# Gates kept in DRAM, high weight parts first, three weight buffers, two sums in the convolution and a new order of products in a hybrid decoder step

## The chip, the cores and the metric

The kernel runs on one core of one Trainium2 chip. The metric is the device time of one execution in microseconds (us). Five engines matter: PE (TensorE: matmuls, transposes), DVE (VectorE), ACT (ScalarE: activations, copies), POOL (GpSimd: elementwise work) and SP (SyncE: it issues nearly all DMAs, in one queue). Each runs its own instructions in order, and they wait for each other on semaphores.

## What is computed

One step of a decoder layer on 520 tokens (512 of a prompt, 8 samples), 1024 features. Three mixers run side by side on the columns of one projection, and each has a gate:

```python
h = rms_norm(x, g_mix)
proj = jnp.einsum('ntd,de->nte', h, w_in)
u_a, z_b, u_c, gate_in = ...                       # 1024, 1024, 512, 3072 columns
c_a, new_conv_a = causal_dwconv(u_a, conv_a, w_conv_a, b_conv_a)          # width 4
y_a, new_h = rg_lru(c_a, h_a, ...)                                         # A: gated recurrence
glu_b = z_b[..., :W_B] * jax.nn.sigmoid(z_b[..., W_B:])
c_b, new_conv_b = causal_dwconv(glu_b, conv_b, w_dw_b, b_dw_b)             # B: width 31
y_b = jax.nn.silu(layer_norm(c_b, ln_g_b, ln_b_b))
y_c, ... = s5_ssm(u_c, s_re, s_im, ...)                                    # C: diagonal SSM, then GLU
```

Each y is projected to 1024 features (w_pa, w_pb, w_pc), multiplied by sigmoid(gate_in + b_gate) of its branch, and the three are added. Then come w_out, the residual, RMSNorm, a SwiGLU FFN of width 2816 with its residual, and a last RMSNorm.

## The kernel before

**Layout and products.** Features lie on the 128 partitions, the 520 tokens on the free axis, as two halves of 260 columns. Both operands of a large product are split exactly into a high and a low part in float32r, and three products are added: high weight by high input, high weight by low input, low weight by high input. `prod` (L232) goes over the k tiles of 128 rows; for each it calls `prod1` (L240), which issues the three products for two halves: 6 matmuls per k, 48 for 8 k tiles, 24 for 4 (L244). One such group makes one tile of 128 output columns in a PSUM tile of the pool mm, which has three.

**Weights.** `wcol` loads two column tiles with one DMA on SP's queue (`wload`, L209, 1 MB, two buffers wraw). `wsplit` makes whi on ACT (L216) and wlo on DVE or, for the keys in ON_POOL, on POOL (L217). There are two whi and two wlo buffers, so a tile can be split only when the product two before is done.

**Steps.** The order of TensorE's work is written by hand in the string ORDER (L43); each word calls a function of the table `step`. DVE, ACT, POOL and SP are ordered by a scheduler, by priorities. The words:
- b0.*, b1.*: first products of branch B and its GLU, which fill the convolution's inputs `gext`. bs: states of the samples. bc.t: the convolution of tile t (`b_conv`, called by `b_low` with the lowest priority).
- cp, cq, cr, cd, cm, ci, co: the S5 recurrence in four groups ct. cr transposes coefficients (L841), cd and cm make and shift the products inside a chunk (L876), ci enters the chunk inputs (L887) and starts the recurrence on DVE, co makes outputs (L951). gelu and glu end branch C; ct transposes C (L720), s0 the samples' states.
- a, ac, ag, ar: inputs, convolution, gates and recurrence of branch A; asp splits its outputs ya (`split`, L247 on ACT, L248 on DVE or POOL) for pa.
- gc.c, ga.c, gb.c: the 24 gate tiles (`gate`); sigmoid into a tile of four, kept in SBUF. pc.c, pa.c, pb.c: the projections (`proj`), which multiply with the gate (in place) and add to the merged sum (L1245, L1247). lnp, ln1, ln2, ln3: the layer norm of branch B.

**The convolution.** For each of four tiles `b_conv` multiplies the samples' windows (L1172), lets ACT make tap 0 into `acc`, and then runs 30 instructions on DVE (L1176), each `acc = window * weight + acc`. Tile t's sum lies in the input of the tile before it, so the order of the tiles is fixed, and the first tap waits for the mark that ci.3 sets (`b_after[0] = marks[3]`).

Of the kernel before, what the change touches and what calls it, by code (L numbers as in the profile page):

```python
# [1566 lines left out]
```

## Time and profile before

| what | value |
|---|---|
| time, median of 3 runs | 943.68 us (942.58 to 943.85) |
| span of the profiled execution | 940.4 us |
| PE busy | 864.3 us (92%), 7329 matmuls |
| DVE busy | 609.5 us (65%), 942 instructions |
| ACT busy | 347.6 us (37%) |
| POOL busy | 289.5 us (31%) |
| DMA | 87.99 MB, mean 94 GB/s |
| chain that ended last | PE 61%, DVE 12% of the span |

The span runs from the first to the last instruction of the profiled execution; the run's time holds a little more. Matmuls are pipelined, so their busy time overlaps and is no measure of pace; the pace is read from start to start, or from a long unbroken piece of the chain. A wait is the idle time of an engine before an instruction, put down to what released it. Instructions of a timeline row ("x5") follow each other without a gap.

### The profile page before, as it was taken

The numbers are of one execution on the slowest core, as the hardware profiler recorded it, in microseconds if no ns is written. First come the engines' busy times: TensorE is split into PE (matmuls) and PEld (weight loads), VectorE is DVE, ScalarE is ACT, GpSimd is POOL, SyncE is SP. The second block draws the span as 40 slices with busy tenths as digits, with TensorE's granted clock in tenths as the row PEclk, the third lists the DMA queues.
The fourth block names the chain that finished last, engine by engine and source line by source line (L and its number), as shares of the span: only waits on it lengthen the run. The fifth ranks groups of instructions, "written<-read, shape, count | busy, mean of one in ns | idle before, by whom it ended". The sixth has DMA issues, their size and how long they took to land.

```text
span 940.4 us, 17346 instructions
## 1 busy us (share of the span) xinstructions
PE 864.3 (92%) x7329; PEld 853.8 (91%) x7329; DVE 609.5 (65%) x942; ACT 347.6 (37%) x516; POOL 289.5 (31%) x363
## 2 busy tenths in 40 slices
PE   6888767957798799999999999999999999999997
PEld 5887767957798699999999999999999999999997
DVE  7899695889999999993546454444442244444453
ACT  6522234627484623223634342333321222223331
POOL 6569994648674441242121210000000000000021
PEclk9998998979799899999999999999999999999999
DMA  6814212130202032222226223333123432321232
GB/s 195 262 57 136 68 51 64 45 114 1 68 24 90 24 133 91 90 91 90 75 72 232 95 85 101 121 100 99 41 84 90 145 98 91 112 91 43 84 99 91
DMA packets 97756, 87.99 MB, mean 94 GB/s; under 512 B 7923, under 2 KB 95207, under 8 KB 97151
## 3 DMA queue, kind: packets, MB, share of 16 engines
q1 hardware_dynamic: 97343, 86.28, 28.3%
q8 instruction: 57, 0.93, 0.4%
q0 software_dynamic: 320, 0.57, 0.2%
q14 instruction: 20, 0.16, 0.1%
q10 hardware_dynamic: 16, 0.03, 0.0%
HBM read 81.23 MB, written 6.19 MB: 93 GB/s over the span
## 4 chain that ended last, share of the span: by engine, by line
PE 61%; DVE 12%; issue 1%; ACT 1%; DVEq 0%
PE mm L244 57%; DVE q L1176 4%; PE mm L1516 3%; DVE t L1176 2%; DVE h L248 1%; DVE wlo L217 1%; DVE q L1109 1%; ACT t L135 0%; DVE tx L1040 0%; DVE t L574 0%; DVE q L1110 0%; DVE q L1245 0%; PE ms L1356 0%; DVE t L1098 0%; PE mm L1187 0%
## 5 line engine op out<-in xcount | busy, mean ns | idle before, releaser
L244 PE MATMUL mm<-q,whi 128*128 128x260 f32 x3296 | 534.3, 284 | 1.6 <-ACT whi L216 1.6
L244 PEld LDWEIGHTS mm<-q,whi 128*128 128x128 f32 x3296 | 454.8, 190 | 2.0 <-ACT whi L216 1.8
L244 PE MATMUL mm<-q,wlo 128*128 128x260 f32 x1648 | 333.1, 283 | 10.1 <-DVE wlo L217 7.1
L216 ACT ACTIVATE whi<-wraw 128x1024 fp32r<-128x1024 f32 (+3 forms) x146 | 139.5, 956 | 433.1 <-PE mm L244 367.9
L244 PEld LDWEIGHTS mm<-q,wlo 128*128 128x128 f32 x1648 | 255.8, 190 | 12.0 <-DVE wlo L217 8.4
L217 DVE TENSOR_TENSOR wlo<-wraw,whi 128x1024 fp32r<-128x1024 f32 (+3 forms) x113 | 127.3, 1127 | 49.4 <-ACT whi L216 49.1
L244 PE MATMUL mm<-h,whi 128*128 128x260 f32 x800 | 130.9, 286 | 2.6 <-DVE h L248 2.5
L1388 POOL TENSOR_TENSOR t<-t,t 128x260 f32<-128x260 f32 (+1 forms) x9 | 8.8, 976 | 369.3 <-ACT t L1386 369.3
L244 PEld LDWEIGHTS mm<-h,whi 128*128 128x128 f32 x800 | 111.5, 191 | 3.1 <-DVE h L248 2.7
L217 POOL TENSOR_TENSOR wlo<-wraw,whi 128x1024 fp32r<-128x1024 f32 (+1 forms) x33 | 71.7, 2173 | 129.5 <-ACT whi L216 114.0
L244 PE MATMUL mm<-h,wlo 128*128 128x260 f32 x400 | 82.0, 287 | 6.3 <-DVE wlo L217 6.0
L244 PEld LDWEIGHTS mm<-h,wlo 128*128 128x128 f32 x400 | 62.7, 192 | 6.9 <-DVE wlo L217 6.4
L1176 DVE SCALAR_TENSOR_TENSOR q<-q,vec 128x512 f32<-128x512 f32 x60 | 59.1, 985 | 1.2
L1467 DVE TENSOR_TENSOR t<-mm,t 128x520 f32<-128x520 f32 x22 | 15.4, 699 | 67.4 <-PE mm L244 58.3
L1457 DVE TENSOR_TENSOR t<-mm,t 128x520 f32<-128x520 f32 x22 | 15.4, 700 | 63.4 <-PE mm L244 63.4
L129 ACT ACT_TABLE_LOAD x23 | 29.5, 1283 | 1.1 <-PEq L1555 0.7
L1176 DVE SCALAR_TENSOR_TENSOR t<-q,vec,t 128x512 f32<-128x512 f32 x30 | 28.4, 945 | 0.4
L1482 DVE TENSOR_TENSOR q<-mm,q 128x520 f32<-128x520 f32 x12 | 8.4, 698 | 27.9 <-PE mm L244 27.9
L1307 POOL TENSOR_TENSOR t<-t,t 128x520 f32<-128x520 f32 x7 | 12.4, 1770 | 41.7 <-ACT t L1306 41.7
L1176 DVE SCALAR_TENSOR_TENSOR q<-q,vec,q 128x512 f32<-128x512 f32 x30 | 24.3, 810 | 0.8
L1245 DVE TENSOR_TENSOR q<-mm,q 128x520 f32<-128x520 f32 x24 | 16.6, 690 | 12.1 <-PE mm L244 12.1
L135 ACT ACTIVATE t<-t,zero_t 128x520 f32<-128x520 f32 x30 | 21.2, 719 | 0.0
(422 smaller groups left out, 1001.8 us busy)
## 6 DMA issues: line engine op xcount, KB each, us to landing
wraw<-w_ffn_in SPq DMA_DIRECT2D x22, 1024.0 KB
wraw<-w_in SPq DMA_DIRECT2D x21, 1024.0 KB
wraw<-w_ffn_out SPq DMA_DIRECT2D x16, 384.0 KB
wraw<-w_ffn_out SPq DMA_DIRECT2D x16, 320.0 KB
wraw<-w_pa SPq DMA_DIRECT2D x4, 1024.0 KB
wraw<-w_out SPq DMA_DIRECT2D x4, 1024.0 KB
xT_d<-q SPq DMA_DIRECT2D x2, 1040.0 KB
q<-xT_d SPq DMA_DIRECT2D x2, 1040.0 KB
```

The costliest lines, as they stand in the source:

```text
L129: last_tab[0] = after(S.preload_act_table_set(SETS[func]), last_tab[0])
L135: last_tab[0] = after(S.activation(out, x, func, **kw), last_tab[0])
L216: S.activation(hi, raw, AF.Copy)
L217: e.tensor_tensor(lo, raw, hi.bitcast(F32), op=ALU.subtract)
L244: T.matmul(ps[:, h, 0:HN], w, x[:, h * HN:(h + 1) * HN], start=first and i == 0, stop=last and i == 2)
L248: e.tensor_tensor(lo, src, hi.bitcast(F32), op=ALU.subtract)
L1176: ins = V.scalar_tensor_tensor(pv(acc), win(k), wdw(k, t), pv(acc), op0=ALU.mult, op1=ALU.add)
L1245: V.tensor_tensor(hv(g), ev(ps), hv(g), op=ALU.mult)
L1307: G.tensor_tensor(ssum, ssum, sq, op=ALU.add)
L1457: V.tensor_tensor(hv(sl), ev(ps), hv(R2), op=ALU.mult)
L1467: V.tensor_tensor(hv(up), ev(ps), hv(R2), op=ALU.mult)
L1516: T.matmul(ps[:, 0, 0:HN], w[:, k, :], x[:, h * HN:(h + 1) * HN], start=j == 0 and k == 0 and i == 0, stop=j == 1 and k == hk - 1 and i == 2)
```

## The change

- `gate` writes its sigmoid into a tile of its own and stores it to a DRAM tensor `g_d`; `proj` loads gate tiles back, up to three ahead, and multiplies there. The merged sums get own tiles (`mg`). That makes 24 stores and 24 loads of 128x520 float32 on SP's queue. The pool of large tiles goes from 11 to 10.
- `prod` issues all products with whi first (high and low input for each k), then all with wlo.
- whi and wlo get three buffers each.
- `b_conv` keeps two sums, `acc` for even and `odd` for odd taps. ACT starts both (taps 0 and 1), DVE runs 29 taps and one add. The sums lie in spare tiles. The mark of ci.3 is no longer waited for (AFTER3 is False).
- ORDER is new: bs comes later, b1.* earlier; gc.0 to ga.5 and gb.0 to gb.5 come earlier, between the steps of S5 and ahead of pa; pb comes last without gates between.
- Code for a convolution on TensorE (CONV_PE, b_shift) is added, but CONV_PE is empty, so none of it is issued.

```diff
 ORDER = """
-bs b0.0 cp.0 as b0.1 ct s0 cp.1 ap b1.0 cr.0 b0.2 b1.1 cd.0 cq.1 ci.0 cr.1 b0.3 b1.3 cm.0 cq.0 ci.1 a.0 a.1 a.2
-ac.0 cd.1 cp.2 co.0 cq.2 ac.1 cm.1 a.3 cr.2 ag.0 co.1 cd.2 ag.1 ac.2 ar.0 b1.2 ci.2 a.4 a.5 ac.3 cm.2 cp.3 gc.0
-gc.1 cr.3 co.2 cd.3 ag.2 cq.3 cm.3 ci.3 ag.3 bc.0 ac.4 ar.1 gc.2 gc.3 ac.5 a.6 co.3 ag.4 ag.5 bc.1 ar.2 a.7 bc.2
-gc.4 bc.3 gelu gc.5 ac.6 gc.6 ag.6 glu.0 glu.1 gc.7 ac.7 glu.2 glu.3 ga.0 ag.7 ar.3 asp pc.0 ga.1 pc.1 pc.2 pc.3
-pc.4 pc.5 ga.2 ga.3 ga.4 pc.6 pc.7 ga.5 gb.0 lnp pa.0 pa.1 gb.1 pa.2 pa.3 pa.4 ga.6 pa.5 ga.7 pa.6 ln1 gb.2 gb.3
-ln2 pa.7 ln3 gb.4 gb.5 pb.0 pb.1 gb.6 gb.7 pb.2 pb.3 pb.4 pb.5 pb.6 pb.7
+b0.0 cp.0 as b0.1 ct ap s0 bs cp.1 b1.0 b1.1 cr.0 b0.2 cq.1 b0.3 ci.0 cr.1 gc.0 gc.1 cq.0 b1.2 cd.0 b1.3 cm.0 a.0 ci.1
+a.2 ac.0 a.1 cd.1 a.3 a.4 ac.1 gc.2 co.0 cp.2 gc.3 cm.1 cr.2 ag.0 cq.2 co.1 cd.2 ag.1 ac.2 ci.2 a.5 cp.3 ac.3 gc.4
+gc.5 cm.2 cr.3 co.2 cd.3 ag.2 ar.0 gc.6 gc.7 cq.3 ci.3 cm.3 ga.0 ga.1 ag.3 ga.6 ga.7 a.6 a.7 bc.0 ac.4 ac.5 ar.1 ga.2
+ga.3 ag.4 ag.5 bc.1 ar.2 bc.2 ga.4 ga.5 co.3 gb.4 ac.6 gb.5 gelu ag.6 glu.0 glu.1 ac.7 glu.2 glu.3 gb.0 gb.1 ag.7 pc.0
+pc.1 ar.3 pc.2 bc.3 pc.3 asp pc.4 pc.5 gb.2 pc.6 pc.7 gb.3 lnp pa.0 pa.1 pa.2 pa.3 ln1 gb.6 gb.7 ln2 pa.4 pa.5 pa.6
+ln3 pa.7 pb.0 pb.1 pb.2 pb.3 pb.4 pb.5 pb.6 pb.7
 """
...
-        hi, lo = dst or (wp.tile([P, nk, P], F32R, tag="whi", name=nm("whi")),
-                         wp.tile([P, nk, P], F32R, tag="wlo", name=nm("wlo")))
+        hi, lo = dst or (wp.tile([P, nk, P], F32R, tag="whi", name=nm("whi"), bufs=3),
+                         wp.tile([P, nk, P], F32R, tag="wlo", name=nm("wlo"), bufs=3))
...
-        n = len(xk)
-        for k, (xh, xl) in enumerate(xk):
-            prod1(ps, hi[:, k, :], lo[:, k, :], xh, xl, first and k == 0, last and k == n - 1)
...
+        mms = [(hi[:, k, :], x) for k, xx in enumerate(xk) for x in xx]
+        mms += [(lo[:, k, :], xx[0]) for k, xx in enumerate(xk)]
+        n = len(mms)
+        for i, (w_, x) in enumerate(mms):
             for h in range(2):
-                T.matmul(ps[:, h, 0:HN], w, x[:, h * HN:(h + 1) * HN], start=first and i == 0, stop=last and i == 2)
+                T.matmul(ps[:, h, 0:HN], w_, x[:, h * HN:(h + 1) * HN], start=first and i == 0, stop=last and i == n - 1)
...
-        S.activation(pv(acc), win(0), AF.Identity, bias=wdw(31, t), scale=wdw(0, t))
-        for k in range(1, 31):
-            ins = V.scalar_tensor_tensor(pv(acc), win(k), wdw(k, t), pv(acc), op0=ALU.mult, op1=ALU.add)
...
+            odd = tt()
+            S.activation(pv(acc), win(0), AF.Identity, bias=wdw(31, t), scale=wdw(0, t))
+            S.activation(pv(odd), win(1), AF.Copy, scale=wdw(1, t))
+            for k in range(2, 31):
+                x = pv((acc, odd)[k % 2])
+                ins = V.scalar_tensor_tensor(x, win(k), wdw(k, t), x, op0=ALU.mult, op1=ALU.add)
+                if k == 2 and t in b_after:
+                    after(ins, b_after[t])
+            ins = V.tensor_tensor(pv(acc), pv(acc), pv(odd), op=ALU.add)
...
-        tact(hv(gt[br, c // 4][:, c % 4, :]), ev(ps), AF.Sigmoid, bias=vb("b_gate", 8 * br + c))
-
-    mx = []
+        g = tt()
+        tact(hv(g), ev(ps), AF.Sigmoid, bias=vb("b_gate", 8 * br + c))
+        Y.dma_start(g_d[br, c], g)
+
+    mx, mg = [], {}
+    ahead = [(br, c) for br in (2, 0, 1) for c in range(8)]
 
     def proj(br, wname, nk, xk, c):
+        while ahead and len(gt) < 3:
+            n = ahead.pop(0)
+            gt[n] = tt()
+            Y.dma_start(gt[n], g_d[n[0], n[1]])
...
-        m, g = gt[2, c // 4][:, c % 4, :], gt[br, c // 4][:, c % 4, :]
-        V.tensor_tensor(hv(g), ev(ps), hv(g), op=ALU.mult)
+        m, g = mg[c // 4][:, c % 4, :], gt.pop((br, c))
+        V.tensor_tensor(hv(m if br == 2 else g), ev(ps), hv(g), op=ALU.mult)
```

On PE before, these rows stand from cd.1 (L863) over co.0 (L951) to cm.1 (L876, transposes of t, which POOL and DVE make from cd.1's result):

```order
L863 MATMUL ms_198_1749<-h_111_1061,q_66_683 32x128 x8
L951 MATMUL mm_211_1794<-h_129_1167 32x136 x4
L951 MATMUL mm_211_1794<-h_148_1329,h_168_1505 32x136 x8
L951 MATMUL mm_211_1794<-h_129_1167 32x128 x4
L951 MATMUL mm_211_1794<-h_148_1329,h_168_1505 32x128 x8
L951 MATMUL mm_211_1794<-h_129_1167 32x128 x4
L951 MATMUL mm_211_1794<-h_148_1329,h_168_1505 32x128 x8
L951 MATMUL mm_211_1794<-h_129_1167 32x128 x4
L951 MATMUL mm_211_1794<-h_148_1329,h_168_1505 32x128 x8
L876 MATMUL ms_221_1873<-ident_80,t_199_1758 128x128 x4
```

On PE after, directly ahead of cm.1 (now L894) stands the product of gc.3; three more whole products (a.3, a.4, gc.2) and co.0 lie between it and cd.1. These are the product's last rows, from the eighth group of its high weights on:

```order
L252 MATMUL mm_242_2205<-q_22_152,whi_240_2201 128x260 x2
L252 MATMUL mm_242_2205<-q_20_150,whi_240_2201 128x260 x2
L252 MATMUL mm_242_2205<-q_22_152,whi_240_2201 128x260 x2
L252 MATMUL mm_242_2205<-q_20_150,whi_240_2201 128x260 x2
L252 MATMUL mm_242_2205<-q_22_152,whi_240_2201 128x260 x2
L252 MATMUL mm_242_2205<-q_19_149,wlo_241_2202 128x260 x8
L252 MATMUL mm_242_2205<-q_20_150,wlo_241_2202 128x260 x8
L894 MATMUL ms_244_2257<-ident_80,t_211_1930 128x128 x4
L859 MATMUL ms_246_2264<-ident_80,h_229_2169 128x128 x4
```

Four products of 48 matmuls came between cd.1 and cm.1, and within a product wlo (the last 16 matmuls) now comes after all of whi.

On DVE before, the taps begin behind the end of ci.3 (L907); t_330 is the only sum of the first tile:

```order
L907 TENSOR_TENSOR h_319_2634<-h_316_2621 128x4x128
L1176 SCALAR_TENSOR_TENSOR t_330_2687<-q_74_808,vec_147,t_330_2687 128x2x256
L217 TENSOR_TENSOR wlo_353_2895<-wraw_351_2892,whi_352_2894 128x1024
L1176 SCALAR_TENSOR_TENSOR t_330_2687<-q_74_808,vec_147,t_330_2687 128x2x256
L1042 SCALAR_TENSOR_TENSOR t_348_2883<-q_73_802,vec_147,tx_347_2879 128x2x256
L1048 SCALAR_TENSOR_TENSOR t_348_2883<-q_73_802,vec_147,tx_347_2879 128x2x4
L1176 SCALAR_TENSOR_TENSOR t_330_2687<-q_74_808,vec_147,t_330_2687 128x2x256
```

On DVE after, the same place; t_382 and t_385 are the two sums, wlo_400 the low weights of ga.2:

```order
L227 TENSOR_TENSOR wlo_377_3262<-wraw_375_3259,whi_376_3261 128x1024
L227 TENSOR_TENSOR wlo_400_3471<-wraw_398_3468,whi_399_3470 128x1024
L1202 TENSOR_TENSOR t_383_3372<-q_72_801,vec_147 128x248
L1206 TENSOR_REDUCE t_384_3374<-t_383_3372 128x8
L1061 SCALAR_TENSOR_TENSOR t_387_3414<-q_75_804,vec_147,tx_386_3410 128x2x256
L1067 SCALAR_TENSOR_TENSOR t_387_3414<-q_75_804,vec_147,tx_386_3410 128x2x4
L1236 TENSOR_SCALAR t_382_3371<-t_384_3374,vec_147 128x2x4
L1229 SCALAR_TENSOR_TENSOR t_382_3371<-q_72_801,vec_147,t_382_3371 128x2x256
L1229 SCALAR_TENSOR_TENSOR t_385_3376<-q_72_801,vec_147,t_385_3376 128x2x256
L1229 SCALAR_TENSOR_TENSOR t_382_3371<-q_72_801,vec_147,t_382_3371 128x2x256
```

The taps alternate between two tiles, and the low weights of ga.2 stand ahead of the first.

On SP before, the loads between the weights of the RG-LRU gates (w_rg) and the projections follow each other:

```order
L1066 DMA t_397_3435<-w_rg 128x2x128
L1066 DMA t_397_3435<-w_ig 128x2x128
L209 DMA wraw_406_3462<-w_glu_c 128x4x256
L209 DMA wraw_424_3601<-w_glu_c 128x4x256
L209 DMA wraw_434_3672<-w_in 128x8x256
L209 DMA wraw_454_3802<-w_pc 128x4x256
L209 DMA wraw_464_3919<-w_pc 128x4x256
```

On SP after, the same place; g_d is the DRAM tensor of the gates:

```order
L1294 DMA g_d_813<-t_406_3580 128x520
L219 DMA wraw_464_4073<-w_glu_c 128x4x256
L219 DMA wraw_479_4158<-w_glu_c 128x4x256
L1294 DMA g_d_813<-t_432_3789 128x520
L1294 DMA g_d_813<-t_436_3846 128x520
L1294 DMA g_d_813<-t_442_3956 128x520
L219 DMA wraw_488_4228<-w_in 128x8x256
L1085 DMA t_455_4045<-w_rg 128x2x128
L1085 DMA t_455_4045<-w_ig 128x2x128
L1294 DMA g_d_813<-t_450_4025 128x520
L219 DMA wraw_505_4367<-w_pc 128x4x256
```

Stores of gates came in between, up to three ahead of one weight load.

## Rows read from the trace of the kernel before

**Rows 1.** Busy time of each engine by stretch (us, with counts), clock, DMA share, GB/s.

```profile
0.00:70.00 70.00, 56.31 (x413) 52.77 (x414) 57.89 (x245) 31.68 (x73) 43.08 (x95) 0.98 0.55 173
70.00:146.97 76.97, 54.08 (x509) 52.85 (x507) 66.92 (x90) 18.09 (x30) 72.82 (x111) 0.89 0.31 97
146.97:222.00 75.03, 64.62 (x677) 62.81 (x678) 59.02 (x88) 36.62 (x60) 41.05 (x55) 0.91 0.16 51
222.00:250.00 28.00, 16.89 (x190) 15.95 (x189) 27.89 (x30) 16.84 (x22) 24.27 (x27) 0.86 0.15 48
250.00:367.40 117.40, 105.56 (x816) 103.52 (x816) 115.54 (x137) 64.64 (x91) 54.78 (x44) 0.93 0.20 66
367.40:940.40 573.00, 566.80 (x4731) 565.94 (x4731) 282.25 (x356) 179.75 (x242) 53.48 (x33) 1.00 0.30 97
```

**Rows 2.** The chain that ended last: start us, us, what.

```profile
367.41 68.69 PE mm L244 x572
...
657.87 226.63 PE mm L244 x1896
```

**Rows 3.** Waits of PE over the whole span: us, times, longest.

```profile
PE mm L244 <- DVE wlo L217: 13.1, 7, 6.0
PE ms L876 <- DVE t L866: 12.3, 1, 12.3
PE ms L841 <- DVE h L771: 9.1, 1, 9.1
PE mm L887 <- POOL h L849: 9.1, 2, 4.8
```

**Rows 4.** The taps up to 367.41 us: duration ns min/median/max, first and last start.

```profile
L1176 DVE SCALAR_TENSOR_TENSOR t<-q,vec,t x30: 737/748/1810, 231.6 to 289.0; 128x512 f32<-128x512 f32 x30
...
L1176 DVE SCALAR_TENSOR_TENSOR q<-q,vec,q x22: 739/752/1664, 344.3 to 367.3; 128x512 f32<-128x512 f32 x22
```

**Rows 5.** Groups of DVE by shape: busy us, mean ns of one | idle before.

```profile
L217 DVE TENSOR_TENSOR wlo<-wraw,whi 128x1024 fp32r<-128x1024 f32 x80 | 98.9, 1237 | 17.4 <-ACT whi L216 17.1
L1176 DVE SCALAR_TENSOR_TENSOR q<-q,vec 128x512 f32<-128x512 f32 x60 | 59.1, 985 | 1.2
L1176 DVE SCALAR_TENSOR_TENSOR t<-q,vec,t 128x512 f32<-128x512 f32 x30 | 28.4, 945 | 0.4
L1176 DVE SCALAR_TENSOR_TENSOR q<-q,vec,q 128x512 f32<-128x512 f32 x30 | 24.3, 810 | 0.8
...
L248 DVE TENSOR_TENSOR h<-q,h 128x520 fp32r<-128x520 f32 x8 | 9.8, 1234 | 0.0
```

**Rows 6.** The same chain, two taps of one tile.

```profile
287.45 0.76 DVE t L1176
288.24 0.76 DVE t L1176
```

**Rows 7.** Timeline of DVE at 365 us: start us, us, instruction.

```profile
365.48 0.74 DVE L1176 SCALAR_TENSOR_TENSOR q<-q,vec,q 128x512 f32<-128x512 f32 x1
366.13 1.22 DVE L217 TENSOR_TENSOR wlo<-wraw,whi 128x1024 fp32r<-128x1024 f32 x1
```

**Rows 8.** Timeline of PE at cm.1 (L876).

```profile
146.97 1.09 PE L876 MATMUL ms<-ident,t 128*128 128x128 f32 x4 [12.32 <-DVE t L866]
147.71 1.22 PE L244 MATMUL mm<-q,whi 128*128 128x260 f32 x4
```

**Rows 9.** Timeline of PE at cr.3.

```profile
203.87 1.94 PE L841 MATMUL ms<-ident,h 128*128 128x128 f32 x8 [9.13 <-DVE h L771]
```

**Rows 10.** The last stretch behind a 1 MB load, columns as in rows 1.

```profile
246.90:247.90 1.00, 0.00 (x0) 0.00 (x0) 1.00 (x1) 0.00 (x0) 1.00 (x2) 1.00 0.29 93
```

**Rows 11.** Timeline of DVE at 279 us.

```profile
279.75 3.48 DVE L1176 SCALAR_TENSOR_TENSOR t<-q,vec,t 128x512 f32<-128x512 f32 x2
```

**Rows 12.** Timeline of POOL over the same time.

```profile
279.23 1.74 POOL L217 TENSOR_TENSOR wlo<-wraw,whi 128x512 fp32r<-128x512 f32 x1
```

**Rows 13.** Waits of SP's queue: us, times, longest.

```profile
SPq L209 <- DVE wlo L217: 546.4, 73, 31.2
```

More of the change, by code (lines that the diff above doesn't have):

```diff
@@ L183, in loads_g @@
         seq("g", G.dma_start(vrow[124:128, 0, :], a["b_dw_b"][0].rearrange("(t p) -> t p", p=P)))
+        if CONV_PE:
+            seq("g", G.memset(vrow[96:128, 2, 96:128], 0.0))
+            for kk in range(8):
+                n = 4 if kk < 7 else 3
+                Y.dma_start(vrow[16 * kk:16 * kk + 16, 2, 0:32 * n].rearrange("r (s c) -> r s c", c=32),
+                            a["w_dw_b"][0, 4 * kk:4 * kk + n].rearrange("s (r c) -> r s c", c=32))
         for ri, n in enumerate(("b_ssm_re", "b_ssm_im")):
@@ L309, in vec_t @@
         V.tensor_copy(vec[:, 0, :], ps[:, 0, :])
+        if CONV_PE:
+            ps = ms((P, P))
+            T.transpose(ps, vrow[:, 2, :], ident)
+            V.tensor_copy(wq, ps)
+    if CONV_PE:
+        wq = tt([P, P])
     def vb(name, i):
@@ L325, in hybrid_step @@
     uc_w = [(ht([P, 8, P], F32R), ht([P, 8, P], F32R)) for _ in range(2)]
-    uc_w += [tuple(wp.tile([P, 8, P], F32R, tag=tag, name=nm(tag)) for tag in ("whi", "wlo")) for _ in range(2)]
+    uc_w += [tuple(wp.tile([P, 8, P], F32R, tag=tag, name=nm(tag), bufs=3) for tag in ("whi", "wlo")) for _ in range(2)]
     def uc_hi(c, d):
@@ L980, in c_glu @@
         split(sg, *ycx[e_])
+    gext = [qt([P, 2, 1096]) for _ in range(2)]
     uext = [qt([P, 4, 548]) for _ in range(2)]
@@ L1121, in a_split @@
         return res
-    gext = [qt([P, 2, 1096]) for _ in range(2)]
     fin_b = cst.tile([P, 152], F32, name="fin_b")
@@ L1159, in hybrid_step, with b_shift @@
     b_after = {}
+    gsh = {}
+    def b_shift(t):
+        g = gext[t // 2][:, t % 2, :]
+        gs = gsh[t] = qt([P, 4, 540])
+        G.memset(gs[96:128, :, 539:540], 0.0)
+        for s_ in range(4):
+            n = 540 if s_ < 3 else 539
+            for q in range(4):
+                Y.dma_start(gs[32 * s_:32 * s_ + 32, q, 0:n], g[32 * q:32 * q + 32, s_:s_ + n])
+    spare = []
     def b_conv(t):
         g = gext[t // 2][:, t % 2, :]
-        acc = cbt[t] = tt() if t == 0 else gext[(t - 1) // 2][:, (t - 1) % 2, 0:NT]
+        on_pe = t in CONV_PE
+        acc = cbt[t] = g[:, 0:NT] if on_pe else spare.pop() if spare else tt()
         def win(k):
@@ L1180, in b_conv @@
-        b_after[t + 1] = ins.ins.name
+        sm = tt([P, 8])
+        V.tensor_reduce(sm.rearrange("p (h b) -> p h b", h=2), pr.rearrange("p (h b) k -> p h b k", h=2),
+                        axis=mybir.AxisListType.X, op=ALU.add)
+        if on_pe:
+            gs = gsh.pop(t)
+            cw = [tt([P, 4, 4, 32]) for _ in range(2)]
+            for i in range(2):
+                w = wq.rearrange("p (k t q) -> p t k q", t=4, q=4)[:, t, 4 * i:4 * i + 4]
+                V.tensor_tensor(cw[i], mask.unsqueeze(1).unsqueeze(1).to_broadcast([P, 4, 4, 32]),
+                                w.unsqueeze(3).to_broadcast([P, 4, 4, 32]), op=ALU.mult)
+            ps = mm()
+            for kk in range(8):
+                for q in range(4):
+                    T.matmul(ps[32 * q:32 * q + 32, 0, :], cw[kk // 4][:, kk % 4, q, :], gs[:, q, 4 * kk:4 * kk + 512],
+                             start=kk == 0, stop=kk == 7)
+            S.activation(pv(acc), ps[:, 0, :].rearrange("p (h n) -> p h n", h=2), AF.Identity, bias=wdw(31, t))
+        else:
+            odd = tt()
[7 more added lines that the diff above has]
+            ins = V.tensor_tensor(pv(acc), pv(acc), pv(odd), op=ALU.add)
+            for t2 in range(t + 1, 4):
+                b_after[t2] = ins.ins.name
+            spare.append(g[:, 0:NT])
@@ L1182, in hybrid_step @@
+        V.tensor_scalar(sv(acc), sm.rearrange("p (h n) -> p h n", h=2), wdw(31, t), None, op0=ALU.add)
     ones_t = cst.tile([P, P], F32, name="ones_t")
@@ L1225, in ln_out @@
             ybx.append((yh[:, t, :], yl[:, t, :]))
+    g_d = dr.tile([3, 8, P, NT], F32, name="g_d")
     gt = {}
     def gate(br, c):
-        if c % 4 == 0:
-            gt[br, c // 4] = qt([P, 4, NT])
         w = wcol(w_in, "in", 20 + 8 * br + c, 8)
@@ L1260, in b_low @@
     def b_low(t):
-        if t == 0:
-            b_after[0] = marks[3]
+        if 3 in marks and AFTER3:
+            b_after.setdefault(t, marks[3])
         with tc.high_priority(offset=-100000):
@@ L1273, in hybrid_step @@
         "gelu": c_gelu, "glu": c_glu,
-        "bs": b_states, "b0": lambda t: sgs.__setitem__(t, b_in(t)), "b1": lambda t: b_in1(t, sgs.pop(t)), "bc": b_low,
+        "bs": b_states, "b0": lambda t: sgs.__setitem__(t, b_in(t)), "b1": lambda t: b_in1(t, sgs.pop(t)), "bg": b_shift, "bc": lambda t: b_conv(t) if t in CONV_PE else b_low(t),
         "as": a_states, "ap": a_pre, "s0": load_s0, "a": a_in, "ac": a_conv, "ag": a_gates, "ar": a_rec,
```

23 lines of the change are left out of this document (11 added, 12 removed).

## The prediction

> **What bounds the kernel now.** The profiled execution has a span of 940.4 us; the median of the runs is 943.68, so 3.3 us lie outside the span, and I add them at the end. I read first the busy time by stretch [rows 1]. From 367.4 us to the end PE is busy for 566.8 of 573.0 us at clock 1.00, and DVE for 282.3: there TensorE is the only bound. Ahead of it no engine is full all the time, but from 222 to 367.4 us DVE is busy for 27.9 + 115.5 = 143.4 of 145.4 us, while PE has gaps. The chain of waits says the same in order of time [rows 2]: up to 367.41 us it runs mostly through DVE's convolution taps (L1176), from there through PE's products without a break; 1896 matmuls take 226.63 us, 119.5 ns each, which is my price of a matmul of 260 columns. So the time is **the moment at which DVE stops holding TensorE, plus the TensorE work that is left at that moment**. Now that is 367.4 + 573.0. The waits of PE [rows 3] come last: 12.3 us for t of L866, 9.1 for h of L771, 9.1 for h of L849, 13.1 for DVE's low weight parts. Nearly all of them lie ahead of 367 us. They are not worth their face value: an earlier PE only reaches the DVE-bound stretch earlier, and what counts is what DVE does by its end and how much PE can put in front of it.
>
> **TensorE's new order.** Before, the product of ga.5 is the last that waits for DVE (its low weights, 367.41 us, after 4 of its 48 matmuls). Products of pc are already behind it; ga.5 to ga.7 and gb.0 to gb.7, eleven of the 24 gates, come later. In the new order only gb.6 and gb.7 are left behind the place where I expect DVE to let go, which is pa.0: its inputs ya come from the recurrence and its weights are loaded late, and it is the last product whose inputs stand behind most of the taps in DVE's order. With the high parts first, pa.0 needs the low part of its last input at its 31st matmul. So ahead of that place stand nine products more (ga.5 to ga.7, gb.0 to gb.5) and 30 matmuls of pa.0, less the 4 of ga.5 that were done: 9 x 48 + 26 = 458 matmuls x 119.5 ns = 54.7 us that PE does earlier. What is left then is 573.0 - 54.7 = 518.3 us. The pieces of PE work are the same in kind and number, so nothing else is added there.
>
> **What DVE must have done by then.** By 367.4 us DVE has worked for 327.3 us (the sum of its first five stretches [rows 1]), so it has stood idle for 40.1. In its new order, up to the last input of pa.0, I count against what it did by 367.4 us:
> - Taps: 106 instead of 81 (82 had started, the last at 367.3 [rows 4]). The 120 taps take 111.8 us, 0.93 each [rows 5]. With two sums the taps of a tile alternate. A tap right behind one that writes the same tile starts 0.79 us after it (287.45, 288.24 [rows 6]); another instruction starts 0.65 us after a tap (365.48, 366.13 [rows 7]). I count 57 taps in the timeline directly behind one of their own sum; 57 x about 0.125 = 7 us over 120 taps, or 0.06 each. So 106 x 0.87 - 81 x 0.93 = 16.9 us.
> - Low weight parts: seven more of 1024 elements on DVE, 7 x 1.24 [rows 5] = 8.7.
> - Low parts of ya: eight h instead of four, 4 x 1.23 [rows 5] = 4.9.
> - The gate products of pc (eight, where seven sums L1245 were), the adds of the two sums and the sample column's start: at 0.7 and less each, together about +3.4. ACT takes tap 1 as it took tap 0 four times more, on an engine that works 64.6 of 117.4 us there [rows 1]: nothing on the path.
>
> The sum is 33.9 us. If DVE stands idle as long as before, it reaches the place at 367.4 + 33.9 = 401.3 us. Will it? The waits that go would make it earlier: ci.0 and ci.1 (L849, 9.1 us in two) and cm.1 (12.32 us at 146.97 us, then four matmuls in 1.22 us [rows 8], about half the pace) get one to five whole products more between themselves and what they wait for; in front of cm.1 only co.0's small matmuls stood before. But something new comes: in DVE's order the first tap stands behind the low weights of ga.2, and these may be written only when the product three before, ga.7, is done, so DVE waits for PE there although a third buffer was added. PE's path to it: the transposes of cr.3 still wait for DVE (L771, at 203.87 us now [rows 9]); by the order DVE has some 10 us less work ahead of them, so about 194; then 388 matmuls and transposes, by their rows some 41 us, and an estimated 5 us in which ag.2 waits for DVE's next pieces: 240. Before, the first tap started at 231.6 [rows 4]. From there DVE has some 162 us of work to the place: 402. Two ways, one number. I take 401.3.
>
> **The other edits.** The wait of a product for its low weights, 13.1 us where DVE makes them [rows 3], moves from its 5th to its 33rd matmul, 3.3 us later; but the last input comes due at the 31st instead of the 45th, 14 x 119.5 ns = 1.7 us earlier, so where an input is last (glu.0, pc.0, pa.0) up to 1.7 us is lost; at pa.0 it is in the sum. bs goes behind s0, ct and b1 move: they lie far ahead of the DVE-bound stretch, and by the longest single waits of PE after the first products, other than those at cm and cr, 4.8 and 6.0 us [rows 3], I bound it by -5 and +5 and take 0. Gates in DRAM: 24 stores and 24 loads of 266 KB on SP's queue. A 1 MB load issued at 242.90 us is moved by 247.9 (its last stretch has a DMA share of 0.29 [rows 10]), so a gate's tile takes some 1.3 us of the DMA engines' time, and the whole 48 some 62 us in a stretch where they are 0.2 to 0.3 busy [rows 1]: hidden. What it may cost in waits is a rival.
>
> The forecast is then 401.3 + 518.3 + 3.3 = **922.9 us**, rounded to 923, 2.2% less.
>
> **A rule against two sums.** The rows show 0.79 us against 0.65 between starts [rows 6, 7]. The Trainium skill (VectorE: DVE Perf Modes, section "The DRAIN you can't avoid") says that the next operation does not start until the pipe is empty, and that chaining without semaphores does not skip this. By that rule two sums would bring nothing, the taps would cost 106 x 0.93, 6.4 us more, and the time would be 929 us. The trace speaks against it: the instruction behind a tap of 0.74 us starts after 0.65. It changes the forecast within its range only.
>
> **Rivals.**
> 1. DVE comes earlier. The removed waits shorten DVE's idle time, 10.0 us from 70 to 147 and 16.0 from 147 to 222 [rows 1]; if half of it goes and ga.7 is done in time, DVE arrives 13 us earlier: 910 us. For it: 21 us of PE waits end there. Against it: the wait for ga.7's buffer gives it back.
> 2. The taps become dearer. Some 19 taps now take 1.67 to 1.8 us or more because POOL works beside them (279.75, two taps in 3.48 us [rows 11], while a split on POOL takes 1.74 [rows 12]). More gates in front mean other POOL splits beside the taps. Ten more such taps are 10 us: 933. Twenty more, and the gain is gone, 943: "no change", the more so as ln1 now follows pa.3 instead of pa.6 and DVE's sums for it have 17 us less cover.
> 3. SP's queue, the slower end. A gate's store waits for ACT's sigmoid, and all weight loads behind it in the queue wait with it; loads of gates wait for a free tile in the same way. Now SP waits 546.4 us in 73 waits for DVE's L217 [rows 13], so a load goes out as soon as its buffer is free. That is three products of 48 matmuls, 17 us, ahead of need, and with the 5 us that it takes [rows 10] 12 us are to spare. If stores and gate loads hold each of the 25 weight loads between the first gate and pb back by more than these 12 us, PE waits for the excess each time: an excess of 0.8 us, 20 us in all, eats the gain (943), one of 1.5 us gives 923 + 37 = 960 us. So it decides from a delay of about 13 us, a good two products, for each load. For it: stores of two or three gates stand in a row ahead of one load. Against it: PE has done the product of such a gate before the buffers of that load come free, and ACT is half idle.
> 4. The change does not do what it says: the gates do not run ahead, since ag.4, ag.6 and glu.0 in front of them stop PE first. PE then still does them before 401 us if its own work fits: 160 us from 240 on for the roughly 990 matmuls up to the place, 118 us. That leaves 42 us of waits free, so the time stays 923: a part of the forecast, with no chance of its own.
>
> **How the numbers follow.** The forecast, 915 to 931, has 0.52; rival 1, near 910 and down to 904, 0.22; rival 2 near 933 has 0.12 and as no change 0.06; rival 3 has 0.08. Two parts in a thousand, 1.9 us, are about what a measurement of this kernel can tell from no change. Faster is 0.52 + 0.22 + 0.12 = 0.86, same 0.06, slower 0.08. The range holds the forecast, most of rival 1 and rival 2's 933 to 940: 904 to 940.
>
> **What would show it.** Right: PE without a wait at L894 (cm) and at ci's products; the first tap near 240 us behind a DVE wait for PE; back-to-back taps 0.65 to 0.70 us apart; gaps of PE from about 240 to 400 us, all for DVE; PE unbroken from pa.0 on, with about 518 us left. Wrong: PE waiting for whi or for a DMA between 150 and 400 us (rival 3); many taps at 1.7 us (rival 2); PE-bound already before 390 us (rival 1); long waits at ln1, ln2 or pb.0, which I hold at nothing.

## The result and the profile after

The changed kernel takes **928.66 us** (median of 4 runs, 926.78 to 929.07) against 943.76 us (942.58 to 944.74) of the kernel before, run beside it: a ratio of 0.983, 95% interval 0.9815 to 0.9845. It is 1.6% faster, 15.1 us of the 20.7 that were forecast, and lies inside the range. The profiled span is 926.6 us, 2.1 us less than the median.

The same view of stretches as [rows 1] (busy us and counts of PE, weight loads, DVE, ACT, POOL; clock; DMA share; GB/s), now for the kernel after:

```profile
70.00:146.97 76.97, 76.97 (x667) 76.30 (x666) 59.41 (x79) 25.41 (x37) 67.89 (x102) 1.00 0.26 83
146.97:222.00 75.03, 68.38 (x773) 64.95 (x773) 54.52 (x89) 38.67 (x61) 44.16 (x59) 0.95 0.30 91
222.00:250.00 28.00, 28.00 (x236) 28.00 (x235) 22.59 (x23) 10.77 (x14) 23.47 (x25) 1.00 0.37 120
250.00:367.40 117.40, 89.77 (x758) 88.09 (x758) 115.49 (x148) 67.78 (x96) 65.20 (x44) 0.88 0.24 81
367.40:926.60 559.20, 547.25 (x4528) 545.23 (x4527) 287.41 (x363) 180.52 (x241) 57.07 (x45) 0.99 0.33 108
```

From 70 to 147 us PE was busy for 54.1 us at clock 0.89 [rows 1]; now it is full at 1.00. By 367.4 us it has issued 2811 matmuls where it had issued 2605, and 4528 are left where 4731 were. The gain is made ahead of 250 us. From 250 to 367.4 us PE does less than before (758 matmuls for 816), and DVE is as full as it was.

The waits of PE over the whole span (us, times, longest), to be laid beside [rows 3]:

```profile
PE mm L252 <- ACT t L258: 24.1, 4, 11.4
PE mm L252 <- DVE wlo L227: 4.0, 1, 4.0
PE mm L252 <- DVE h L259: 3.6, 1, 3.6
PE ms L859 <- DVE h L789: 3.0, 1, 3.0
```

The 12.3 us at cm.1 and the 9.1 us at ci have no row any more, the 9.1 us at cr.3 are 3.0, and the 13.1 us for low weights of DVE are 4.0. In their place stands one new line, 24.1 us for split parts t of branch A's gates (at ag.4 and ag.6 their weights). The timeline of PE shows where (start, us, instruction, idle time before it and its releaser):

```profile
281.11 4.69 PE L252 MATMUL mm<-t,t 128*128 128x260 f32 x24 [11.36 <-ACT t L258]
...
302.38 4.11 PE L252 MATMUL mm<-q,whi 128*128 128x260 f32 x32 [2.26 <-ACT t L138]
...
323.98 1.24 PE L252 MATMUL mm<-t,t 128*128 128x260 f32 x4 [9.84 <-ACT t L258]
...
332.71 2.94 PE L252 MATMUL mm<-h,whi 128*128 128x260 f32 x10 [3.56 <-DVE h L259]
...
378.64 2.10 PE L252 MATMUL mm<-h,wlo 128*128 128x260 f32 x8 [4.05 <-DVE wlo L227]
...
488.62 0.50 PE L252 MATMUL mm<-q,whi 128*128 128x260 f32 x2 [0.63 <-ACT q L258]
489.36 0.51 PE L252 MATMUL mm<-q,whi 128*128 128x260 f32 x2 [0.23 <-DVE q L259]
```

281.11 is ag.4, 323.98 ag.6, 378.64 the low weights of pc.4. Behind 378.64 PE runs without a gap but for the small one at the first product of w_out. So the shape is the forecast one, gaps between 270 and 379 us and then only TensorE, but two things differ from it. The gaps end at 379 us and not at pa.0, and the two longest wait for ACT's splits of branch A; only those at 332.71 and 378.64, 7.6 us, wait for DVE directly.

Where DVE begins its taps (timeline of DVE):

```profile
246.84 1.57 DVE L227 TENSOR_TENSOR wlo<-wraw,whi 128x1024 fp32r<-128x1024 f32 x1 [4.99 <-PE mm L252]
...
250.30 3.15 DVE L1229 SCALAR_TENSOR_TENSOR t<-q,vec,t 128x512 f32<-128x512 f32 x3
...
293.33 0.75 DVE L1229 SCALAR_TENSOR_TENSOR t<-q,vec,t 128x512 f32<-128x512 f32 x1
293.99 0.74 DVE L1229 SCALAR_TENSOR_TENSOR q<-q,vec 128x512 f32<-128x512 f32 x1
294.65 0.74 DVE L1229 SCALAR_TENSOR_TENSOR t<-q,vec,t 128x512 f32<-128x512 f32 x1
...
403.94 0.68 DVE L259 TENSOR_TENSOR h<-q,h 128x520 fp32r<-128x520 f32 x1
```

The wait of 4.99 us is the forecast one: the low weights of ga.2 wait for PE to finish ga.7. Taps of the two sums start 0.66 us apart. The first tap was forecast near 240 us. The last row is the last low part of ya, the input of pa.0 that the prediction held to be last.

### The profile page after: what moved, and what is told of

It reads as the page before. It is cut to its first block, busy times and chain, and to the rows that moved or that the text cites. A ratio compares the mean times of both kernels' runs of the same rounds, so it can differ in the third digit from the quotient of the medians.

```text
span 926.6 us, 17538 instructions
## 1 busy us (share of the span) xinstructions
PE 866.2 (93%) x7329; PEld 854.6 (92%) x7329; DVE 598.2 (65%) x942; ACT 355.1 (38%) x519; POOL 299.2 (32%) x363
## 4 chain that ended last, share of the span: by engine, by line
PE 76%; DVE 16%; POOL 3%; issue 2%; ACT 1%; DMA 1%; SPq 0%; DVEq 0%; ACTq 0%; POOLq 0%
PE mm L252 69%; DVE t L1229 4%; PE mm L1581 3%; DVE q L1229 2%; DVE wlo L227 1%; PE mm L969 1%; DMA t<-w_ig 1%; DVE tx L1059 1%; DVE s_t L592 1%; PE mm L905 1%; DMA q<-x_prompt 1%; DVE s_n L601 1%; DVE h L259 1%; DVE q L1129 0%; POOL h L352 0%
## 5 line engine op out<-in xcount | busy, mean ns | idle before, releaser
L252 PE MATMUL mm<-q,whi 128*128 128x260 f32 x3296 | 420.4, 285 | 5.2 <-ACT t L138 2.3
L252 PEld LDWEIGHTS mm<-q,whi 128*128 128x128 f32 x3296 | 406.9, 190 | 7.2 <-ACT t L138 2.9
L252 PE MATMUL mm<-q,wlo 128*128 128x260 f32 x1648 | 215.4, 282 | 0.0
L252 PEld LDWEIGHTS mm<-q,wlo 128*128 128x128 f32 x1648 | 204.5, 188 | 0.0
L252 PE MATMUL mm<-h,whi 128*128 128x260 f32 x800 | 108.2, 290 | 4.4 <-DVE h L259 3.6
L1229 DVE SCALAR_TENSOR_TENSOR t<-q,vec,t 128x512 f32<-128x512 f32 x71 | 61.4, 883 | 0.0
L252 PE MATMUL mm<-h,wlo 128*128 128x260 f32 x400 | 57.1, 289 | 4.0 <-DVE wlo L227 4.0
L252 PE MATMUL mm<-t,t 128*128 128x260 f32 x96 | 17.3, 338 | 24.8 <-ACT t L258 24.1
L138 ACT ACTIVATE t<-mm,vec 128x520 f32<-128x520 f32 x44 | 30.0, 689 | 19.6 <-PE mm L252 16.5
L1229 DVE SCALAR_TENSOR_TENSOR q<-q,vec 128x512 f32<-128x512 f32 x30 | 31.0, 1035 | 0.0
L592 DVE TENSOR_TENSOR t<-t,t 128x520 f32<-128x520 f32 x30 | 20.8, 699 | 0.7
```

The source lines that it names most:

```text
L138: last_tab[0] = after(S.activation(out, x, func, **kw), last_tab[0])
L252: T.matmul(ps[:, h, 0:HN], w_, x[:, h * HN:(h + 1) * HN], start=first and i == 0, stop=last and i == n - 1)
L592: V.tensor_tensor(out, x, y, op=ALU.mult)
L1229: ins = V.scalar_tensor_tensor(x, win(k), wdw(k, t), x, op0=ALU.mult, op1=ALU.add)
```

## The experiments

The theory: PE's time at the end is the moment when DVE lets go, and each part of the change acts by what it does to DVE's way up to there. The rivals are named in each expectation. All ratios are against the kernel before, run beside each (943.7 to 944.8 us); differences in us are against the 928.66 of the change.

### One part undone

**Two sums.** `u_sum` makes one sum again (ACT starts tap 0, DVE adds 30 taps).

```diff
-            S.activation(pv(odd), win(1), AF.Copy, scale=wdw(1, t))
-            for k in range(2, 31):
-                x = pv((acc, odd)[k % 2])
+            for k in range(1, 31):
+                x = pv(acc)
...
-            ins = V.tensor_tensor(pv(acc), pv(acc), pv(odd), op=ALU.add)
```

> The changed kernel with one sum per convolution tile again (30 taps on DVE, no add). Theory (the end is DVE's arrival at pa.0 plus the TensorE work left): dependent taps cost 0.79 us from start to start instead of 0.66, four taps come back from ACT and four adds go, so DVE arrives 5 to 9 us later and the time goes from 928.7 to 934 to 938. Rival (the pipe empties after every DVE operation, whether it depends or not): at most +3 us, 929 to 931.

Measured: 936.58 us (934.21 to 937.62), ratio 0.9917 (0.9904 to 0.9931), so the second sum is worth 7.9 us. The time lies in the theory's range, and the rival falls. The groups of DVE by shape, first the one-sum kernel, then the change (busy us, mean ns):

```profile
L1227 DVE SCALAR_TENSOR_TENSOR q<-q,vec 128x512 f32<-128x512 f32 x60 | 58.9, 981 | 1.5
L1227 DVE SCALAR_TENSOR_TENSOR q<-q,vec,q 128x512 f32<-128x512 f32 x30 | 31.4, 1045 | 0.6
L1227 DVE SCALAR_TENSOR_TENSOR t<-q,vec,t 128x512 f32<-128x512 f32 x30 | 25.6, 854 | 0.5
```

```profile
L1229 DVE SCALAR_TENSOR_TENSOR t<-q,vec,t 128x512 f32<-128x512 f32 x71 | 61.4, 883 | 0.0
L1229 DVE SCALAR_TENSOR_TENSOR q<-q,vec 128x512 f32<-128x512 f32 x30 | 31.0, 1035 | 0.0
L1229 DVE SCALAR_TENSOR_TENSOR q<-q,vec,q 128x512 f32<-128x512 f32 x15 | 14.2, 946 | 0.2
```

115.9 us for 120 taps against 106.6 for 116. The price is not paid at pa.0: from 250 to 400 us PE issues 1024 matmuls in this kernel, 964 in the change. It is paid one place later: with one sum the layer norm's first column sums (ln1) wait for DVE, in the timeline of PE of that kernel:

```profile
430.33 2.07 PE L1240 MATMUL mm<-t,ones_t 128*128 128x260 f32 x4 [12.01 <-DVE t L1246]
```

**High parts first.** `u_hif` goes back to three products for each k.

```diff
-        mms = [(hi[:, k, :], x) for k, xx in enumerate(xk) for x in xx]
-        mms += [(lo[:, k, :], xx[0]) for k, xx in enumerate(xk)]
+        mms = [m for k, (xh, xl) in enumerate(xk)
+               for m in ((hi[:, k, :], xh), (hi[:, k, :], xl), (lo[:, k, :], xh))]
```

> The changed kernel with the products of a k tile together again (high, high, low weight by k). Theory: waits for low weights come back (7 of 13 us on TensorE before), but lie in the stretch that DVE bounds, and last inputs come due 1.7 us later, so 926 to 932. Rival (high parts first is what takes TensorE's waits away): the 16 us of waits for low weights come back in full, 938 to 945.

Measured: 936.10 us (935.06 to 938.71), ratio 0.9919 (0.9905 to 0.9933): 7.4 us lost. The theory's range is missed; the rival's is just not reached.

**Third buffers.** `u_buf` gives whi and wlo two buffers each (`bufs=3` taken out).

> The changed kernel with two whi and two wlo buffers again. Theory: DVE's wait ahead of the first tap is for the product two before instead of three, one product of 5.7 us later, and DVE arrives that much later at pa.0: 932 to 936. Rival (buffers make no difference, since DVE is late anyway): 928 to 930. Second rival (splits run less ahead everywhere and TensorE waits for whi too): over 940.

Measured: 942.72 us (940.93 to 944.53), ratio 0.9987 (0.9979 to 0.9996): 14.1 us lost, nearly all of the gain. The theory's range (932 to 936) is missed; the second rival's, over 940, is met.

**Order and DRAM alone.** `only_ord` is the three edits in one: one sum, products by k, two buffers. It keeps the dropped mark of ci.3 and the pool of ten large tiles, which no run undoes by themselves.

> The changed kernel with one sum, products by k and two buffers: what is left of the change is the order and the gates in DRAM. Theory: the order carries the 54.7 us of TensorE work in front, the rest some 10 to 14 us: 936 to 943. Rival (the order is all of it): 928 to 931. Rival (the order is worth nothing without the buffers): 945 or more.

Measured: 951.81 us (951.2 to 953.97), ratio 1.0084 (1.0071 to 1.0098). What is left makes the kernel slower than before by 8 us, as the second rival has it (the order is worth nothing without the buffers). The three parts, undone singly, cost 7.9 + 7.4 + 14.1 = 29.4 us, together 23.2: they overlap.

**The old order with the rest.** `u_ord` keeps all edits but takes the old ORDER (a gate is loaded back only once it is stored).

> The changed kernel with the order of the kernel before (gates still through DRAM, loaded ahead only once stored). Theory (the order puts TensorE work in front of DVE's stretch and is the largest part): 936 to 944, what stays is the two sums and a little of the buffers. Rival (undoing the sums, the high-first products or the buffers cost 7 to 14 us each, so those carry the gain): 928 to 932.

Measured: 960.91 us (957.66 to 962.19), ratio 1.0177 (1.016 to 1.0194): 32 us above the change, 17 above the kernel before. That undoing the order costs most was expected; the size was far off, and both ranges are missed. Its first tap comes early, at 220.81 us, and PE's last wait for DVE ends at 334 us, but by then too little has been done: busy times in its last stretch, columns as above,

```profile
367.40:956.80 589.40, 582.18 (x4847) 580.75 (x4845) 275.54 (x341) 189.08 (x250) 52.05 (x34) 1.00 0.34 109
```

4847 matmuls are left where 4528 are left in the change. The waits at cm.1 (7.5 us) and ci (5.1) are back. Why the edits cost the old order 17 us against the kernel before was not tried.

**What the early waits do.** The four kernels in the stretches ahead of the taps; in turn the change, `u_hif`, `u_buf`, `only_ord`, each at 146.97 to 250 us:

```profile
146.97:250.00 103.03, 96.38 (x1007) 92.95 (x1007) 77.11 (x111) 49.45 (x74) 67.63 (x83) 0.97 0.32 99
```

```profile
146.97:250.00 103.03, 93.36 (x973) 90.49 (x972) 80.85 (x112) 47.21 (x73) 64.96 (x84) 0.93 0.30 94
```

```profile
146.97:250.00 103.03, 89.40 (x930) 86.31 (x928) 75.23 (x109) 45.76 (x70) 59.62 (x72) 0.92 0.26 83
```

```profile
146.97:250.00 103.03, 89.01 (x946) 85.58 (x946) 76.08 (x111) 45.43 (x71) 64.86 (x84) 0.97 0.29 91
```

By 250 us PE has issued 2051, 1986, 1959 and 1938 matmuls (with 377, 376, 408 and 399 up to 70 us, and 667, 637, 621 and 593 from there to 146.97). It is behind by 65, 92 and 113, which at 119.5 ns each is an estimated 7.8, 11.0 and 13.5 us. DVE's first tap, at 250.30 in the change, comes at 256.88, 260.03 and 264.61: later by 6.6, 9.7 and 14.3 us. In the change DVE stands there for 4.99 us, ahead of the low weights of ga.2. In the two with two buffers it stands there too, later; the first row is `u_buf`, the second `only_ord`:

```profile
252.91 1.60 DVE L227 TENSOR_TENSOR wlo<-wraw,whi 128x1024 fp32r<-128x1024 f32 x1 [4.55 <-issue]
```

```profile
257.63 1.23 DVE L227 TENSOR_TENSOR wlo<-wraw,whi 128x1024 fp32r<-128x1024 f32 x1 [11.38 <-ACT whi L226]
```

In both, DVE waits once more, 2.6 and 3.9 us, for ACT's start of the sum, ahead of which ACT stood 3.1 and 4.1 us for PE in front of high weights. So in the new order PE's early backlog comes back nearly whole as a later first tap; in these two kernels the way leads through weights that wait for PE. The time lost is 7.4, 14.1 and 23.2 us. That the later tap is what carries the loss to the end is argued, not shown. In `u_hif` DVE has no such wait; there its other work ahead of the taps came later. `u_buf` loses some more afterwards, where PE waits 5.9 us for ACT's high weights at 383.56 us.

**Gates without DRAM.** `u_gate` leaves the stores and loads out.

```diff
-        Y.dma_start(g_d[br, c], g)
...
-            Y.dma_start(gt[n], g_d[n[0], n[1]])
+            G.memset(gt[n], 0.5)
```

> The changed kernel without the gates' way through DRAM: the sigmoid is made, but neither stored nor loaded; a tile set to 0.5 by GpSimd stands for it, so the merged sum is not the reference's. Theory (the transfers are hidden): 926 to 930. Rival (stores ahead of weight loads hold SP's queue): 8 to 15 us less, 914 to 921.

Measured: 928.0 us (925.78 to 930.79), ratio 0.9835 (0.9811 to 0.986): no difference. In the change SP waits 96.2 us in 19 waits for ACT's sigmoid ahead of stores, at most 16.2, and without the transfers the time is the same: rival 3 of the prediction falls.

### What holds PE from 250 to 379 us

**Fewer taps.** `x_tap` leaves ten taps of each tile out (`range(2, 21)`).

> The changed kernel with taps 21 to 30 of each convolution tile left out (10 of 29 DVE instructions per tile), so the convolution is not the reference's. Theory (the end is DVE's arrival plus the TensorE work left): 30 to 36 taps less ahead of pa.0, 0.7 to 0.8 us each, so 20 to 28 us less: 901 to 909. Rival (TensorE's gaps at ag.4 and ag.6 come from late weights of the RG-LRU gates, not from DVE's load): at most 8 us less, 920 or more.

Measured: 917.48 us (916.46 to 918.42), ratio 0.9722 (0.9706 to 0.9738): 11.2 us less. Both expectations are missed, the value lies between. 40 taps at the 0.92 us of the groups above are 37 us of DVE's work, and 11 of them reach the end. The waits at ag.4 and ag.6 stay; behind them 0.19 us is left where the change waits 8.4 us in four waits:

```profile
282.81 5.41 PE L252 MATMUL mm<-t,t 128*128 128x260 f32 x24 [12.43 <-ACT t L258]
323.74 1.23 PE L252 MATMUL mm<-t,t 128*128 128x260 f32 x4 [9.51 <-ACT t L258]
...
329.77 3.23 PE L252 MATMUL mm<-h,whi 128*128 128x260 f32 x10 [0.19 <-DVE h L259]
```

So DVE's work is what holds PE behind ag.6. Of ag.4 and ag.6 themselves the run tells little, because DVE's load ahead of them did not fall: taps of the next tile moved up, and by 323.5 us DVE had run 53 taps where the change had run 58, and had worked for 268.2 us against 267.1. What leads to ag.4 in the change reads from the timelines of POOL, ACT and SP in turn:

```profile
272.84 2.33 POOL L1126 TENSOR_TENSOR t<-t,t 128x8 f32<-128x8 f32 x1 [5.89 <-DVE t L592]
275.23 1.12 POOL L1131 COPY q<-t 128x8 f32<-128x8 f32 x1
276.30 1.25 POOL L1133 COPY fin_a<-t 128x8 f32<-128x8 f32 x1
...
308.23 0.19 POOL L1131 COPY q<-t 128x8 f32<-128x8 f32 x1
308.36 0.20 POOL L1133 COPY fin_a<-t 128x8 f32<-128x8 f32 x1
```

```profile
280.43 0.63 ACT L258 ACTIVATE t<-t 128x512 fp32r<-128x512 f32 x1 [6.62 <-DMA t<-w_ig]
```

```profile
278.00 0.47 SPq L1085 DMA_DIRECT2D t<-w_ig  x1
```

DVE's result is late; POOL then needs 4.7 us for three tiny instructions, of which the last two take 0.2 us each elsewhere; only then is a small tile free, SP loads the weights of ag.4's gates into it, ACT and DVE split them, and PE goes on. At ag.6 the way is another: ACT waits 5.7 us for DVE until 315.61 and then runs branch C's activations ahead of the split, which starts at 323.29. Three kernels tried to cut these waits.

**Own tile for these weights.** `x_wrg` loads them into a tile of their own (and has 16 small tiles for 17).

```diff
-                raw, hi, lo = tt([P, 2, 2, P]), tt([P, 2, 2, P], F32R), tt([P, 2, 2, P], F32R)
+                raw = wp.tile([P, 2, 2, P], F32, tag="wrg", name=nm("wrg"), bufs=1)
+                hi, lo = tt([P, 2, 2, P], F32R), tt([P, 2, 2, P], F32R)
```

> The changed kernel with a tile of its own for the raw RG-LRU gate weights (one of the 17 small tiles becomes this one), so that their load at ag.4, which lands just ahead of the end of TensorE's 11.4 us wait, goes out long before. Theory (DVE's work is the bound, the late load sits beside it): 926 to 929. Rival (the queue of SP and the shortage of tiles are what TensorE waits for): the waits at ag.2 and ag.4, 8 to 12 us, go in full: 917 to 921.

Measured: 931.47 us (931.03 to 931.88), ratio 0.9871 (0.9856 to 0.9885), 2.8 us more, so both ranges are missed (what the lacking small tile costs was not measured by itself, and no run has more of them). The load is early, and yet ag.4 waits 9.9 us, since ACT now stands one instruction earlier, for a tile that the same tiny POOL instructions hold:

```profile
280.51 0.70 ACT L138 ACTIVATE t<-mm,vec 128x520 f32<-128x520 f32 x1 [5.36 <-POOL fin_a L1134]
281.11 0.62 ACT L258 ACTIVATE t<-wrg 128x512 fp32r<-128x512 f32 x1
```

The wait at ag.6 halves, to 4.9 us, and the one at glu.0 grows from 3.6 to 6.6.

**Tiny instructions on DVE.** `x_hs` moves them off POOL (`E = V`, and the two copies with them).

> The changed kernel with the samples' small operations of the RG-LRU recurrence (128x8, L1125 to L1133) on DVE instead of GpSimd. On GpSimd beside DVE's taps they took 2.33, 1.12 and 1.25 us at 273 us where they take 0.2 to 0.6 elsewhere, and the weights of ag.4 wait behind them. Theory (DVE's load decides): some 40 operations of about 0.1 us come to DVE, TensorE's 11.4 us wait at ag.4 gets shorter, the time stays at 926 to 931. Rival (the chain over GpSimd holds ag.4 and so the end): 3 to 6 us less, 922 to 925.

Measured: 928.22 us (927.14 to 929.35), ratio 0.9835 (0.9821 to 0.9848): no difference, as the theory has it. At ag.4 the waits are 8.6 + 1.2 us, so POOL's tiny instructions made about 1.5 of the 11.4 us there; at ag.6 they are 9.2 + 4.4.

**ag.4 and ag.5 later.** `e_ag4` puts them behind ga.4 and ga.5.

```diff
-ga.2 ga.3 ag.4 ag.5 bc.1 ar.2 bc.2 ga.4 ga.5
+ga.2 ga.3 ga.4 ga.5 ag.4 ag.5 bc.1 ar.2 bc.2
```

> The changed kernel with ag.4 and ag.5 behind ga.4 and ga.5 in TensorE's order, and bc.1, ar.2, bc.2 behind them. Theory (a wait of TensorE ahead of DVE's arrival is not worth its face value): the 11.4 us wait at ag.4 goes, later waits take its place, 925 to 931. Rival (each wait of TensorE counts): 917 to 920.

Measured: 932.33 us (931.58 to 933.49), ratio 0.9879 (0.9866 to 0.9893), 3.7 us more. The time lies just above the theory's range, and the rival falls. The wait at ag.4 falls to 5.3 us, and from 250 to 400 us PE issues 1048 matmuls where the change issues 964. What it wins is lost again at the layer norm's first sums (ln1), which the change passes without a wait:

```profile
422.71 2.07 PE L1238 MATMUL mm<-t,ones_t 128*128 128x260 f32 x4 [6.61 <-DVE t L1244]
```

So a second limit of DVE's lies close behind pa.0, as in `u_sum`.

**The taps earlier.** `e_bc0` has bc.0 behind cm.0, `e_bc3` behind ag.3.

> The changed kernel with bc.0 moved in the order from behind a.7 to behind cm.0; DVE's first 30 taps then stand from row 267 of its order on instead of 387, among the work of S5. Theory: they fill DVE's idle time from 120 to 250 us (some 40 us), the rest starts with 20 us less to do, and the time falls by 10 to 18 us, to 911 to 919. Rival (the taps push S5's chain back, which TensorE waits for): 928 or more.

> The changed kernel with bc.0 moved in the order from behind a.7 to behind ag.3, four products earlier. In DVE's order the first tap then stands right behind the end of ci.3 (h of L925, at 239 us in the changed kernel), and a dozen taps ahead of the low weights of ga.2, for which DVE waited 5.0 us for TensorE. Nothing of S5 stands behind a tap. Theory (the moment of the first tap, 250.3 us in the changed kernel, sets DVE's arrival): the first tap at 241 to 244 us and the time 5 to 8 us less, 921 to 924. Rival (what DVE wins there it loses again at ag.4 and ag.6): 927 to 930.

Measured: `e_bc0` 945.34 us (943.56 to 946.47), ratio 1.0013 (1.0003 to 1.0023): 16.7 us more than the change, as the rival has it. Its first tap is at 114.05 us, and the taps now stand ahead of S5's work: from 147 to 222 us PE is busy for 57.64 us where it was for 68.38. `e_bc3` 928.77 us (928.6 to 931.82), ratio 0.9839 (0.9826 to 0.9853): no difference, the rival's range. Its first tap comes 4.7 us earlier, so the moment of the first tap does not set the end by itself. Its timeline of DVE:

```profile
245.65 13.44 DVE L1224 SCALAR_TENSOR_TENSOR t<-q,vec,t 128x512 f32<-128x512 f32 x15
259.01 1.21 DVE L222 TENSOR_TENSOR wlo<-wraw,whi 128x1024 fp32r<-128x1024 f32 x1
```

Fifteen taps come first, and the low weights of ga.2 12 us later than in the change (246.84). PE then waits 4.0 us at 274.35 for low weights that POOL makes, and 6.6 + 2.6 us at ag.4. Here the earlier first tap was paid with a late weight.

## Why the prediction was right, and where it was off

**Direction and much of the mechanism held.** The waits at cm and ci went, DVE waited for ga.7 ahead of the first tap, taps lie 0.66 us apart, PE runs unbroken from pa.0 on but for 1.2 us, the gates' transfers are hidden (`u_gate`). Two signs of being wrong came true as well. PE is the only bound from 379 us, and "PE-bound already before 390 us" was to be rival 1's sign. And PE waited at ag.4 behind a DMA (ACT's 6.62 us for w_ig), rival 3's sign, though `u_gate` clears the gates' transfers of it. The gaps were not all for DVE.

**The place, 401.3 us.** The last low part of ya ends at 404.6 us, 3.3 us late. PE, however, does not wait there. It reaches pa.0 at 402.06 and its 31st matmul at 405.7, 1 us after that low part; its last wait was at pc.4 (378.64), 23.4 us ahead of pa.0. So DVE let go at another product and earlier, and it is luck that pa.0's input came just as PE reached it. The working had two errors that cancel, as the view of stretches shows (columns as in [rows 1]):

```profile
0.00:404.60 404.60, 351.27 (x3048) 341.10 (x3049) 347.58 (x628) 190.57 (x299) 256.08 (x333) 0.94 0.36 114
```

DVE did 347.6 us of work up to 404.6 instead of 361.2. Of the 13.6 us 5.5 are eight low parts h<-q,h, two of which serve glu and not ya: they took 6.5 us where the sum held 12.0 (7.1 for four before 367.4, and 4.9). Against that the 107 taps took 97.8 us, 0.91 each and not 0.87, which is some 5 more than the sum held; the rest I have not split up. And DVE stood idle for 57.0 us where I kept the 40.1 of before. The rows above place this ahead of 250 us: 17.6 us from 70 to 147 (10.0 before), 20.5 from 147 to 222 (16.0) and 5.4 from 222 to 250 (0.1). The second way in the prediction, by the first tap, was 10.3 us early: cr.3 came at 198.27 for 194, ga.7's end 2.5 us later than the 41 + 5 us behind it gave, and between 246.84 and the tap at 250.30 lie 3.5 us of other DVE work that I had left out.

**What was left, 518.3 us.** From 405.7 to the end are 520.9 us. Of the 2.6 more, 1.2 (from start to start) are the wait of w_out for its last input, which comes due earlier with high parts first: the price that the prediction named for three other products, found at a fourth. Outside the span 2.1 us lie instead of 3.3. So, with 405.7 for 401.3, the miss is 4.4 + 2.6 - 1.2 = 5.8 us.

**The step that failed: "the other edits".** The third buffers and the high parts first were taken at nothing. In this order they are worth 14.1 and 7.4 us. The sum came out near all the same, because it went by the profile of before plus DVE's work and so assumed in silence that PE would be in time. That PE was in time it owes to these two parts, so the nearness of the sum is in part luck. The reason given for a price of nothing was that PE's early waits only bring PE earlier to a stretch that DVE sets. That fits what happens behind the first tap: `e_ag4` brings PE forward there and gains nothing (`x_wrg` and `x_hs` hardly shortened PE's waits and test it less). It fails ahead of the first tap, as `u_buf` and `u_hif` show. The likely reason is that the prediction itself had put a PE product, ga.7, on DVE's way, and did not carry this back to the waits in front of ga.7.

**The bound was not DVE's load alone.** "DVE is full" made me price the stretch by DVE's work. `x_tap` shows that 37 us less work bring 11, by the waits behind ag.6. The longer waits at ag.4 and ag.6 it does not test, and no single cut at them shortened the time. At ag.4 POOL's slow instructions are about 1.5 us; whether the rest is DVE's fixed order or the shortage of small tiles stays open. And `u_sum` and `e_ag4` show that PE cannot gain much there alone, since ln1 waits for DVE next.

**Two sums** were priced at 6.4 us up to pa.0 and measured at 7.9, but at ln1, which the prediction held at nothing. The rule that the prediction weighed against them (the Trainium skill, VectorE: DVE Perf Modes, section "The DRAIN you can't avoid") would have given nothing for them. The runs disagree with it as I applied it, and it is chance that 929, the time worked out with it, is the time measured. The section also says that an operation which is not held starts earlier, and the 0.66 us agree with that.

**Rival 1** (DVE comes earlier, 910): its sign came, its time did not, and DVE was 3.3 us late at the place. The wait for ga.7, the reason given against it, is there. **Rival 2**: long taps did not become more (17 of 116 took 1.6 us or more, 18 of 120 before), but it saw the thin cover of ln1 rightly: it breaks in `u_sum` (12.0 us). **Rival 4**, gates that do not run ahead, describes 250 to 367.4 us well (758 matmuls for 816), with ag.4 and ag.6 as the stops.
